# Layer 2's feed forward: 19 of 22 up projections as seven half-size block products

## The chip, the cores and the metric

One core of one Trainium2 chip. The time is device microseconds (us) of the whole program, median of three runs; the profile is of one further execution. Engines: PE is TensorE (PEld its weight loads), DVE is VectorE, ACT is ScalarE, POOL is GpSimd, SP issues the transfers.

## The reference

Two layers over 512 latent and 256 context tokens of 1024 features. Each layer mixes tokens and then runs a gated feed forward. Layer 2 computes only the latent tokens, and of it this case concerns the feed forward:

```python
def conv_ffn(h, w_up, conv_w, conv_b, w_down):
    u = h @ w_up
    u = lax.conv_general_dilated(u, conv_w[:, None, :], window_strides=(1,), padding=((1, 1),),
                                 dimension_numbers=('NWC', 'WIO', 'NWC'),
                                 feature_group_count=u.shape[-1]) + conv_b
    a, g = jnp.split(u, 2, axis=-1)
    return (jax.nn.silu(a) * g) @ w_down
```

`w_up` is 1024 x 5632, `w_down` 2816 x 1024, all float32. The convolution runs over three neighbouring tokens, separately for each of the 5632 columns.

## The kernel before

Matrix products keep float32 accuracy with two reduced-precision (fp32r) parts of each operand, h (the rounded value) and l (the rest): each product is three matmuls, h by h, l by h and h by l. The parts are made by a *split*: ACT casts the value to h, and DVE or POOL subtracts h from the value (L477 and L478 in `weight`).

The feed forward (`ffn`) takes the 2816 inner features in 22 blocks j of 128. For one j, `up` handles a *pair* of column blocks of `w_up`, s = 0 for a and s = 1 for the gate's factor. SP loads each block (128 partitions x 8 k x 128, L474), ACT and DVE split it (L477, L478), and PE forms [128 features x 512 tokens] in PSUM, with the weights stationary and the normed features X moving (L1340). In layer 2 that is 2 x 8 x 3 matmuls over 512 columns; for the first two j the 512 columns are two halves, so that work starts before all tokens are there:

```python
ps.append(([(cring.next()[:, 0:256], 0, 512, 256)] if need else []) + ([(pl, 0, 0, 256), (pl, 256, 256, 256)] if j < JS else [(pl, 0, 0, 512)]))
```

The convolution reads PSUM: ACT writes tap 1 and the bias to `cb` (L1345), and DVE adds the two shifted taps (L1346, L1347), each from PSUM and `cb`. Then ACT applies SiLU (L1350), POOL multiplies by the other half (L1351), and ACT and DVE split the product (L1352, L1353). The rows of `w_down` for j are loaded (L1327), cast by ACT (L1329) and split by POOL (L1330).

The blocks form groups of 3, 3, 3, 3, 3, 3 and 4. For a group, `down` multiplies the gated features by the rows of `w_down` for 4 token tiles and 2 halves of the output columns (L488 to L490 in `mm3`; 24 matmuls over 512 columns per j), and DVE adds the 8 results of a group to `fa` (ACT copies those of the first group, L1402; L1404 after). Ahead of each group's down products stands the up projection of the first j of the next group:

```python
pend.append(step(groups[gi + 1][0]))
...
pend += [step(j) for j in groups[gi + 1][1:]]
```

`last_group` does the last down products, and the residual and output follow.

Buffers in layer 2: four raw buffers (two of them `more_raw`), up to six weight buffers (`wr` and `more`, each h and l of 1024 values per partition), one raw buffer and four split ones for the down weights, six for gated features. The features X come from `to_features` (L632, L633 split them), which leaves the unsplit values in the output projection's buffer `mo`. The order of instructions in each engine's queue is fixed when the program is built: a planner lists them by its own cost estimates, and each engine then works through its queue in that order; only layer 2's output projection, ahead of this feed forward, follows an order written by hand. What is not in PSUM lies in SBUF (`arena_f`, `arena_r` and the zones in the profile's names).

## Time and profile before

| | before |
|---|---|
| median of 3 runs | 1800.18 us |
| lowest to highest run | 1798.51 to 1802.9 us |
| span of the profiled execution, first to last instruction | 1798.2 us |
| mean granted TensorE clock (1 is full) | 0.990 |
| PE busy | 1730.8 us (96%) |
| DVE, ACT, POOL busy | 1158.1, 790.7, 540.7 us |
| feed forward of layer 2, first up projection to the end | 1417.3 to 1798.2 us |

The profiled execution's own device time isn't given apart from its span; the span is 0.3 us under the lowest run. Busy time counts what an engine records as running, waits inside an instruction included. Matmuls overlap in the records, so their cost is read from the distance between starts. A row names its line, its engine, the operation, what it writes and reads, the shapes and the count. Behind a row, "idle before" and an arrow say how long the engine stood still before it and what ended that.

### The profile page before, as it was taken

The page shows a single profiled execution, that of the slowest core. Times are in us where ns is not written, and L with a number is a line of the kernel's source. Part 1 is how long each engine was busy: PE and PEld are TensorE (multiplying, and loading weights), DVE is VectorE, ACT ScalarE, POOL GpSimd, SP SyncE. Part 2 cuts the span into 40 slices and gives each one's busy share as a digit, 9 for nine tenths or more (in the row PEclk, how much of TensorE's full clock was granted, in tenths as well). Part 3 has the DMA queues.
Part 4 walks back from the last instruction along what each step waited for, and adds up shares of the span by engine and source line. Part 5 has one row for each costly group of instructions (what it writes and reads, how often), then busy time and mean ns, then how long its engine had stood idle before and what let it go on. Part 6 is the DMA issues. An engine that isn't in the chain of part 4 may idle for free.

```text
span 1798.2 us, 29093 instructions
## 1 busy us (share of the span) xinstructions
PE 1730.8 (96%) x11226; PEld 1450.7 (81%) x11226; DVE 1158.1 (64%) x2356; ACT 790.7 (44%) x1650; POOL 540.7 (30%) x485
## 2 busy tenths in 40 slices
PE   6999999999999999999999998999899999999997
PEld 4888865779898888878788878888778988888886
DVE  5548974662778699775666484499764664545444
ACT  5645444773553323132222355553874553333322
POOL 1325453541330202011120252245542232222223
PEclk9999999999999999999999999999999999999999
DMA  8310144003433335363433332111104353332202
GB/s 312 100 48 25 60 141 153 1 11 107 159 125 111 101 116 152 94 189 93 145 114 92 103 133 73 48 48 48 36 1 138 133 155 102 106 94 82 82 27 91
DMA packets 165582, 177.77 MB, mean 99 GB/s; under 512 B 6998, under 2 KB 137256, under 8 KB 165188
## 3 DMA queue, kind: packets, MB, share of 16 engines
q1 hardware_dynamic: 165156, 173.56, 31.0%
q0 software_dynamic: 288, 2.36, 0.4%
q8 instruction: 88, 1.44, 0.4%
q14 instruction: 50, 0.41, 0.1%
HBM read 165.38 MB, written 10.51 MB: 98 GB/s over the span
## 4 chain that ended last, share of the span: by engine, by line
PE 77%; DVE 13%; DMA 4%; issue 3%; ACT 2%; POOL 0%; DVEq 0%; ACTq 0%; POOLq 0%
PE psum L1340 31%; PE psum L488 10%; PE psum L489 10%; PE psum L490 10%; PE psum L1109 4%; PE psum L1088 3%; DMA arena_f<-in_w_mod 2%; PE psum L1061 2%; PE psum L1062 2%; DVE arena_r L478 1%; PE psum L364 1%; DVE arena_f L1197 1%; DVE arena_f L929 1%; DVE arena_f L423 1%; DMA zone_Z<-in_w_mod 1%
## 5 line engine op out<-in xcount | busy, mean ns | idle before, releaser
L1340 PE MATMUL psum<-zone_Z,arena_r 128*128 128x256 f32 (+1 forms) x2760 | 516.0, 343 | 5.5 <-DVE arena_f L1347 3.8
L1340 PEld LDWEIGHTS psum<-zone_Z,arena_r 128*128 128x128 f32 x2760 | 436.0, 189 | 75.1 <-issue 4.5
L489 PE MATMUL psum<-arena_r,zone_Z 128*128 128x256 f32 (+2 forms) x1124 | 342.2, 305 | 3.6 <-POOL zone_Z L633 2.6
L488 PE MATMUL psum<-arena_r,zone_Z 128*128 128x256 f32 (+2 forms) x1124 | 342.3, 306 | 1.9 <-ACT zone_Z L550 1.0
L490 PE MATMUL psum<-arena_r,zone_Z 128*128 128x256 f32 (+2 forms) x1124 | 341.0, 304 | 0.0
L488 PEld LDWEIGHTS psum<-arena_r,zone_Z 128*128 128x128 f32 x1124 | 212.4, 189 | 18.2 <-issue 6.2
L489 PEld LDWEIGHTS psum<-arena_r,zone_Z 128*128 128x128 f32 x1124 | 213.0, 190 | 17.2 <-issue 3.7
L490 PEld LDWEIGHTS psum<-arena_r,zone_Z 128*128 128x128 f32 x1124 | 212.6, 190 | 13.8 <-issue 5.4
L478 DVE TENSOR_TENSOR arena_r<-arena_f,arena_r 128x1024 fp32r<-128x1024 f32 (+1 forms) x111 | 159.0, 1435 | 87.2 <-ACT arena_r L477 84.8
L477 ACT CAST arena_r<-arena_f 128x1024 fp32r<-128x1024 f32 (+1 forms) x114 | 118.7, 1049 | 145.1 <-PE psum L1340 110.8
L423 DVE SCALAR_TENSOR_TENSOR arena_f<-arena_f 128x256 f32<-128x256 f32 (+1 forms) x224 | 138.8, 657 | 39.3 <-DMA arena_f<-in_w_mod 38.9
L1351 POOL TENSOR_TENSOR arena_f<-arena_f 128x768 f32<-128x768 f32 (+1 forms) x44 | 75.6, 1717 | 278.4 <-DVE arena_f L1347 251.6
L1404 DVE TENSOR_TENSOR arena_f<-arena_f,psum 128x512 f32<-128x512 f32 x100 | 68.2, 683 | 104.9 <-PE psum L490 104.8
L1330 POOL TENSOR_TENSOR arena_r<-arena_f,arena_r 128x1024 fp32r<-128x1024 f32 x22 | 53.8, 2444 | 266.9 <-ACT arena_r L1329 266.9
L1076 POOL TENSOR_SCALAR arena_f<-arena_f 128x768 f32<-128x768 f32 (+3 forms) x96 | 80.1, 837 | 93.5 <-DVE arena_f L1075 90.8
L1073 DVE TENSOR_REDUCE arena_f<-psum 128x1 f32<-128x768 f32 (+4 forms) x120 | 91.1, 767 | 21.8 <-PE psum L1062 20.2
L1330 POOL TENSOR_TENSOR zone_Z<-arena_f,zone_Z 128x1024 fp32r<-128x1024 f32 x22 | 53.9, 2452 | 162.1 <-ACT zone_Z L1329 161.8
L1345 ACT ACTIVATE arena_f<-psum,arena_f 128x512 f32<-128x512 f32 (+1 forms) x132 | 89.0, 701 | 27.8 <-PE psum L1340 27.8
L1346 DVE SCALAR_TENSOR_TENSOR arena_f<-psum,arena_f 128x511 f32<-128x511 f32 (+1 forms) x132 | 84.1, 652 | 20.3 <-ACT arena_f L1345 20.3
L1340 PE MATMUL psum<-zone_Z 128*128 128x512 f32 (+1 forms) x408 | 86.9, 366 | 0.7 <-POOL zone_Z L633 0.6
L1347 DVE SCALAR_TENSOR_TENSOR arena_f<-psum,arena_f 128x511 f32<-128x511 f32 (+1 forms) x132 | 84.8, 655 | 1.5
L1350 ACT ACTIVATE arena_f<-arena_f 128x768 f32<-128x768 f32 (+1 forms) x44 | 32.5, 739 | 120.8 <-DVE arena_f L1347 120.8
(289 smaller groups left out, 3142.9 us busy)
## 6 DMA issues: line engine op xcount, KB each, us to landing
arena_f<-in_ffn_w_up SPq DMA_DIRECT2D x88, 512.0 KB
arena_f<-in_w_mod SPq DMA_DIRECT2D x112, 256.0 KB
arena_f<-in_ffn_w_down SPq DMA_DIRECT2D x44, 512.0 KB
zone_Z<-in_w_mod SPq DMA_DIRECT2D x36, 512.0 KB
arena_f<-in_w_in SPq DMA_DIRECT2D x24, 512.0 KB
arena_f<-in_w_out SPq DMA_DIRECT2D x16, 512.0 KB
xd<-arena_f SPq DMA_DIRECT2D x16, 512.0 KB
arena_f<-xd SPq DMA_DIRECT2D x14, 512.0 KB
```

The lines of the kernel that those rows point to most:

```text
L423: nc.vector.scalar_tensor_tensor(av[:, r], x[:, i], s, av[:, r], ALU.mult, ALU.add)
L477: nc.scalar.copy(hr, rv)
L478: (nc.vector if lo == "v" else nc.gpsimd).tensor_tensor(lr, rv, hf, ALU.subtract)
L488: mm(out, lh, rh, start=first, stop=False)
L489: mm(out, ll, rh, start=False, stop=False)
L490: mm(out, lh, rl, start=False, stop=last)
L1073: nc.vector.tensor_reduce(st[:, 0:1], ps[:, 0:w], AX.X, ALU.max, negate=True)
L1330: nc.gpsimd.tensor_tensor(wp.r[:, 1], rd.f, wp.f[:, 0], ALU.subtract)
L1340: nc.tensor.matmul(p[:, po:po + n], us[s][wi][:, k], X.r[:, xi, k, o:o + n], start=(k == 0 and (wi, xi) == (0, 0)), stop=(k == KT - 1 and ...
L1345: nc.scalar.activation(d, p, AF.Identity, bias=ci[:, 3:4], scale=ci[:, 1:2])
L1346: nc.vector.scalar_tensor_tensor(d[:, 1:n], p[:, 0:n - 1], ci[:, 0:1], d[:, 1:n], ALU.mult, ALU.add)
L1347: nc.vector.scalar_tensor_tensor(d[:, 0:n - 1], p[:, 1:n], ci[:, 2:3], d[:, 0:n - 1], ALU.mult, ALU.add)
```

## The change

From j = 3 on (JD = 3), layer 2's up projection goes through `up7`. The 1024 features are cut into two halves and the 512 tokens into two halves, so the pair of column blocks (s = 0, 1) by feature halves is a 2 x 2 block matrix A, and X is a 2 x 2 block matrix B (`Quad`, four blocks of 512 features x 256 tokens). The product has seven block products in place of eight: four operands on the weights' side are sums (s1 to s4, POOL), four on the tokens' side (T1 to T4) are made once in `token_forms`, half on DVE and half on POOL. Each product is 4 k x 3 matmuls over 256 columns. Three PSUM banks per pair take the products, some accumulating in one bank; ACT copies two results and DVE adds five into `u`, in SBUF, from where the convolution now reads. `gated` is the old end of `up`, cut out as a function.

The buffers change with it: two raw buffers in place of four, four weight buffers of which a pair takes three, two half buffers in the place of a block of X that is no longer read, `fa` in the place of `mo`, four gated buffers. The raw weights are read by one DVE split, one POOL split and the four sums. Pair j = 2 uses two halves of 256 columns, as j = 0 and 1 did. Comments that the diff also removes, the freeing of buffers and `to_features` writing through `Quad.part` are left out here.

```diff
-JS, JL, NLATE = 2, 2, 6
+JS, JD, JL, NLATE = 2, 3, 2, 6
...
+class Quad:
...
+    def __init__(self, mem, at):
+        self.b = [[mem.alloc(2, 4, 256, at=at) for _ in range(2)] for _ in range(2)]
+
+    def part(self, ks, o):
+        b, k, o = self.b[ks.start // 4][o // 256], ks.start % 4, o % 256
+        return (a[:, :, k:k + ks.stop - ks.start, o:] for a in (b.r, b.f))
...
         if not need:
-            self.more = [R.alloc(2, D, at=["Z2"]) for _ in range(2)] + [R.alloc(2, D, at=["Z1"], top=True)]
+            self.forms = [R.alloc(2, 4, 256, at=["Z2"]) for _ in range(2)]
+            self.more = [Buf(R, b.zone, b.ap, b.off, b.n, (2, D)) for b in self.forms] + [R.alloc(2, D, at=["Z1"], top=True)]
...
-        gr = Ring(R, 6, 2, nt)
+        gr = Ring(R, 6 if need else 4, 2, nt)
...
-        fa = F.alloc(NT if need else 4, D)
+        fa = F.alloc(NT, D) if need else self.mo
...
+        js = JS if need else JD
...
-            if j < JS:
+            if j < js:
                 mms.sort(key=lambda m: (m[1][2] + 256) % 768)
             for s, (p, po, o, n), k, wi, xi in mms:
-                nc.tensor.matmul(p[:, po:po + n], us[s][wi][:, k], X.r[:, xi, k, o:o + n], start=(k == 0 and (wi, xi) == (0, 0)), stop=(k == KT - 1 and wi == 1))
+                x = X.r[:, xi, k, o:o + n] if need else X.b[k // 4][o // 256].r[:, xi, k % 4]
+                nc.tensor.matmul(p[:, po:po + n], us[s][wi][:, k], x, start=(k == 0 and (wi, xi) == (0, 0)), stop=(k == KT - 1 and wi == 1))
...
+        def token_forms():
...
+            z = fa.f.rearrange("p (h t) (x k n) -> p h x t k n", h=2, x=2, k=4)
+            b11, b12, b21, b22 = z[:, 0, 0], z[:, 1, 0], z[:, 0, 1], z[:, 1, 1]
+            t1, t2 = (R.alloc(2, 4, 256) for _ in range(2))
+            t3, t4 = self.forms
+            for eng, d, x, y, o in ((nc.vector, b11, b12, b11, t1), (nc.gpsimd, b12, b22, b12, t3), (nc.vector, b22, b22, b11, t2), (nc.gpsimd, b21, b21, b22, t4)):
+                eng.tensor_tensor(d, x, y, ALU.subtract)
+                r, f = (a.rearrange("p i k (t n) -> p i t k n", t=2) for a in (o.r, o.f))
+                nc.scalar.copy(r[:, 0], d)
+                eng.tensor_tensor(r[:, 1], d, f[:, 0], ALU.subtract)
+            st["T"] = [t1, t2, t3, t4]
+
+        def room():
...
+            b12 = X.b[0][1]
+            for b in self.more_raw:
+                b.free()
+            self.raw.bufs, self.raw.k = self.raw.bufs[2:], 0
+            st["big"] = [*wr, more[2]]
+            st["half"] = [b12.part(0, 2, 512), b12.part(1024, 2, 512)]
+            st["S"] = [F.alloc(2, 512) for _ in range(2)]
+            st["u"] = Ring(F, 2, 2, 512)
+            st["c1"] = Ring(F, 2, 256)
+            st["ps"] = PRing(self.PS, [(b ^ 4, 1) for b in (6, 7, 4, 5, 0, 1)])
+            st["k"] = 0
+
+        def split(raw, buf, n, eng):
...
+            hr, hf, lr = buf.r[:, 0, 0:n], buf.f[:, 0, 0:n], buf.r[:, 1, 0:n]
+            nc.scalar.copy(hr, raw)
+            eng.tensor_tensor(lr, raw, hf, ALU.subtract)
...
+        def up7(j):
...
+            raw = [self.raw.next().f for _ in range(2)]
+            for s in range(2):
+                c0 = s * FD + j * P
+                nc.sync.dma_start(raw[s][:, 0:1024].rearrange("p (k n) -> p k n", k=KT), io["ffn_w_up"][L, :, c0:c0 + P].rearrange("(k p) n -> p k n", p=P))
+            a11, a12, a21, a22 = (raw[s][:, i:i + 512] for s in range(2) for i in (0, 512))
+            big = [st["big"][(st["k"] * 3 + i) % len(st["big"])] for i in range(3)]
+            half = st["half"][st["k"] % 2]
+            st["k"] += 1
+            s12, s34 = st["S"]
+            s1, s2, s3, s4 = s12.f[:, 0], s12.f[:, 1], s34.f[:, 0], s34.f[:, 1]
+            A = {}
+            A[1], A[2] = split(raw[0][:, 0:1024], big[0], 1024, nc.vector)
+            nc.gpsimd.tensor_tensor(s1, a21, a22, ALU.add)
+            nc.gpsimd.tensor_tensor(s2, s1, a11, ALU.subtract)
+            A[5], A[6] = split(s12.f.rearrange("p s n -> p (s n)"), big[1], 1024, nc.vector)
+            nc.gpsimd.tensor_tensor(s3, a11, a21, ALU.subtract)
+            nc.gpsimd.tensor_tensor(s4, a12, s2, ALU.subtract)
+            A[7], A[3] = split(s34.f.rearrange("p s n -> p (s n)"), big[2], 1024, nc.gpsimd)
+            A[4], = split(a22, half, 512, nc.gpsimd)
+            rd, wp = rawd.next(), wd.next()
+            nc.sync.dma_start(rd.f, io["ffn_w_down"][L, j * P:(j + 1) * P, :])
+            nc.scalar.copy(wp.r[:, 0], rd.f)
+            nc.gpsimd.tensor_tensor(wp.r[:, 1], rd.f, wp.f[:, 0], ALU.subtract)
+            T = st["T"]
+            B = {1: X.b[0][0], 2: X.b[1][0], 3: X.b[1][1], 4: T[3], 5: T[0], 6: T[1], 7: T[2]}
+            pa, pb, pc = (st["ps"].next()[:, 0:256] for _ in range(3))
+
+            def product(i, ps, first):
+                h, l = A[i]
+                x = B[i].r
+                for k in range(4):
+                    for w, xi in ((h, 0), (l, 0), (h, 1)):
+                        nc.tensor.matmul(ps, w[:, k], x[:, xi, k], start=first and k == 0 and xi == 0 and w is h, stop=k == 3 and xi == 1, skip_group_check=True)
+            u, c1, cb = st["u"].next().f, st["c1"].next().f, cr.next().f
+            add = nc.vector.tensor_tensor
+            c11, c12, c21, c22 = (u[:, s, i:i + 256] for s in range(2) for i in (0, 256))
+            product(1, pa, True)
+            nc.scalar.copy(c1, pa)
+            product(6, pb, True)
+            add(c12, c1, pb, ALU.add)
+            product(5, pc, True)
+            add(c22, c1, pc, ALU.add)
+            product(2, pa, False)
+            nc.scalar.copy(c11, pa)
+            product(7, pb, False)
+            add(c22, c22, pb, ALU.add)
+            product(3, pc, False)
+            add(c12, c12, pc, ALU.add)
+            product(4, pb, False)
+            add(c21, c1, pb, ALU.add)
+            for s in range(2):
+                ci, d, x, n = cw[:, :, s * NJ + j], cb[:, s], u[:, s], 512
+                nc.scalar.activation(d, x, AF.Identity, bias=ci[:, 3:4], scale=ci[:, 1:2])
+                nc.vector.scalar_tensor_tensor(d[:, 1:n], x[:, 0:n - 1], ci[:, 0:1], d[:, 1:n], ALU.mult, ALU.add)
+                nc.vector.scalar_tensor_tensor(d[:, 0:n - 1], x[:, 1:n], ci[:, 2:3], d[:, 0:n - 1], ALU.mult, ALU.add)
+            return gated(cb), wp
...
-            r = up(j)
+            r = up(j) if need or j < JD else up7(j)
```

## Rows read from the trace of the kernel before

**Rows 1.** The page, parts 1 and 4: busy times, and the chain's lines.

```profile
PE 1730.8 (96%) x11226; PEld 1450.7 (81%) x11226; DVE 1158.1 (64%) x2356; ACT 790.7 (44%) x1650; POOL 540.7 (30%) x485
...
PE psum L1340 31%; PE psum L488 10%; PE psum L489 10%; PE psum L490 10%; PE psum L1109 4%; PE psum L1088 3%; DMA arena_f<-in_w_mod 2%; PE psum L1061 2%; PE psum L1062 2%; DVE arena_r L478 1%; PE psum L364 1%; DVE arena_f L1197 1%; DVE arena_f L929 1%; DVE arena_f L423 1%; DMA zone_Z<-in_w_mod 1%
```

**Rows 2.** Busy times by stretch (us), layer 2's feed forward in three stretches.

```profile
core 0: us, PE busy (x) PEld busy (x) DVE busy (x) ACT busy (x) POOL busy (x), PEclk, DMA share, GB/s
1417.30:1451.00 33.70, 33.01 (x243) 31.10 (x242) 23.53 (x35) 21.84 (x35) 12.96 (x8) 1.00 0.54 159
1451.00:1770.00 319.00, 319.00 (x1382) 259.01 (x1381) 155.07 (x175) 110.71 (x144) 77.88 (x41) 1.00 0.27 85
1770.00:1798.20 28.20, 17.73 (x77) 13.96 (x75) 17.12 (x30) 7.80 (x22) 9.55 (x7) 0.85 0.25 93
```

**Rows 3.** TensorE's timeline: start, us covered, line, shape, count merged in the row.

```profile
1449.71 10.65 PE L1340 MATMUL psum<-zone_Z,arena_r 128*128 128x512 f32 x45
...
1429.15 2.92 PE L1340 MATMUL psum<-zone_Z,arena_r 128*128 128x256 f32 x23
...
1252.01 0.28 PE L490 MATMUL psum<-arena_r,zone_Z 128*128 128x256 f32 x1
...
1254.50 0.28 PE L490 MATMUL psum<-arena_r,zone_Z 128*128 128x256 f32 x1
```

**Rows 4.** Instructions by source line, from 1400 us on: ns min/median/max (L1268: whole run).

```profile
L478 DVE TENSOR_TENSOR arena_r<-arena_f,arena_r x22: 1212/2012/2657, 1399.0 to 1710.8; 128x1024 fp32r<-128x1024 f32 x22
...
L1351 POOL TENSOR_TENSOR arena_f<-arena_f x22: 1281/1296/2286, 1444.5 to 1767.9; 128x512 f32<-128x512 f32 x22
...
L1347 DVE SCALAR_TENSOR_TENSOR arena_f<-psum,arena_f x44: 734/749/752, 1439.1 to 1767.0; 128x511 f32<-128x511 f32 x44
...
L1353 DVE TENSOR_TENSOR zone_Z<-arena_f,zone_Z x18: 675/691/2395, 1452.0 to 1769.9; 128x512 fp32r<-128x512 f32 x18
...
L1268 DVE TENSOR_TENSOR arena_f<-psum,arena_f x20: 409/424/425, 420.5 to 1392.5; 128x256 f32<-128x256 f32 x20
```

**Rows 5.** Timelines of POOL (L1330, L1351) and DVE (L1353, L478): start, us.

```profile
1451.42 2.41 POOL L1330 TENSOR_TENSOR zone_Z<-arena_f,zone_Z 128x1024 fp32r<-128x1024 f32 x1
...
1451.98 2.40 DVE L1353 TENSOR_TENSOR zone_Z<-arena_f,zone_Z 128x512 fp32r<-128x512 f32 x1 [1.84 <-ACT zone_Z L1352]
...
1458.70 2.41 POOL L1330 TENSOR_TENSOR arena_r<-arena_f,arena_r 128x1024 fp32r<-128x1024 f32 x1 [4.87 <-ACT arena_r L1329]
...
1459.60 2.58 DVE L478 TENSOR_TENSOR arena_r<-arena_f,arena_r 128x1024 fp32r<-128x1024 f32 x1 [2.64 <-ACT arena_r L477]
...
1463.55 1.22 DVE L478 TENSOR_TENSOR arena_r<-arena_f,arena_r 128x1024 fp32r<-128x1024 f32 x1
...
1463.78 2.13 POOL L1351 TENSOR_TENSOR arena_f<-arena_f 128x512 f32<-128x512 f32 x1 [2.67 <-DVE arena_f L1347]
```

**Rows 6.** L423 (layer 1's modulation): ns min/median/max; timelines of DVE and POOL.

```profile
L423 DVE SCALAR_TENSOR_TENSOR arena_f<-arena_f x224: 466/478/2628, 504.7 to 972.7; 128x256 f32<-128x256 f32 x84, 128x512 f32<-128x512 f32 x28
...
512.02 3.43 DVE L423 SCALAR_TENSOR_TENSOR arena_f<-arena_f 128x256 f32<-128x256 f32 x3 [0.64 <-DMA arena_f<-in_w_mod]
...
512.14 2.62 POOL L1330 TENSOR_TENSOR zone_Z<-arena_f,zone_Z 128x1024 fp32r<-128x1024 f32 x1 [7.47 <-ACT zone_Z L1329]
```

**Rows 7.** SP's timeline, one issue; then busy times by stretch, last column GB/s.

```profile
1481.75 0.37 SPq L474 DMA_DIRECT2D arena_f<-in_ffn_w_up  x1
...
1482.00:1484.00 2.00, 2.00 (x10) 1.65 (x9) 1.13 (x2) 1.22 (x2) 0.00 (x0) 1.00 0.47 134
1484.00:1486.00 2.00, 2.00 (x10) 1.63 (x10) 0.00 (x0) 0.59 (x1) 0.00 (x0) 1.00 0.43 128
```

**Rows 8.** DVE's timeline: the last features of layer 2's feed forward.

```profile
1429.98 1.29 DVE L633 TENSOR_TENSOR zone_Z<-arena_f,zone_Z 128x512 fp32r<-128x512 f32 x2 [1.26 <-ACT zone_Z L632]
```

**Rows 9.** TensorE's timeline, one gap; busy times of the stretch behind it.

```profile
1260.92 0.58 PE L1061 MATMUL psum<-arena_r 128*128 128x256 f32 x1 [2.82 <-ACT zone_Z L1074]
...
1262.00:1270.00 8.00, 7.33 (x55) 6.18 (x55) 6.08 (x21) 5.42 (x14) 6.46 (x10) 0.85 0.00 0
```

More of the change, by code (lines that the diff above doesn't have):

```diff
@@ L631, in to_features @@
         for k4 in (slice(4, 8), slice(0, 4)):
-            h = nc.scalar.copy(X.r[:, 0, k4, off:off + P], zv[:, k4])
-            l = (nc.vector if fast else nc.gpsimd).tensor_tensor(X.r[:, 1, k4, off:off + P], zv[:, k4], X.f[:, 0, k4, off:off + P], ALU.subtract)
+            xr, xf = X.part(k4, off) if isinstance(X, Quad) else (X.r[:, :, k4, off:], X.f[:, :, k4, off:])
+            h = nc.scalar.copy(xr[:, 0, :, 0:P], zv[:, k4])
+            l = (nc.vector if fast else nc.gpsimd).tensor_tensor(xr[:, 1, :, 0:P], zv[:, k4], xf[:, 0, :, 0:P], ALU.subtract)
         self.done[t] = [h, l] if fast else [h, l, e]
@@ L1297, in out_proj @@
         self.wr.k = 0
-        for b in (mo, gb, sq, junk, self.xr, *self.hl):
+        self.mo = mo
+        for b in (gb, sq, junk, self.xr, *self.hl):
             b.free()
@@ L1306, in ffn @@
         nt = NTOK if need else NLAT
+        if not need:
+            self.rc.free()
         wd = Ring(R, 4, 2, D)
         wd.bufs.append(wd.bufs.pop(0))
-        gr = Ring(R, 6, 2, nt)
+        gr = Ring(R, 6 if need else 4, 2, nt)
+        if need:
+            self.mo.free()
         rawd = Ring(F, 1, D)
-        fa = F.alloc(NT if need else 4, D)
+        fa = F.alloc(NT, D) if need else self.mo
         cr = Ring(F, 2, 2, nt)
         lring = self.banks(L, 6, 7, 4, 5)
+        js = JS if need else JD
         cring = self.banks(L, 0, 1)
@@ L1334, in up @@
                 pl = lring.next()
-                ps.append(([(cring.next()[:, 0:256], 0, 512, 256)] if need else []) + ([(pl, 0, 0, 256), (pl, 256, 256, 256)] if j < JS else [(pl, 0, 0, 512)]))
+                ps.append(([(cring.next()[:, 0:256], 0, 512, 256)] if need else []) + ([(pl, 0, 0, 256), (pl, 256, 256, 256)] if j < js else [(pl, 0, 0, 512)]))
             mms = [(s, p, k, wi, xi) for s in range(2) for k in range(KT) for wi, xi in ((0, 0), (0, 1), (1, 0)) for p in ps[s]]
-            if j < JS:
+            if j < js:
                 mms.sort(key=lambda m: (m[1][2] + 256) % 768)
             for s, (p, po, o, n), k, wi, xi in mms:
-                nc.tensor.matmul(p[:, po:po + n], us[s][wi][:, k], X.r[:, xi, k, o:o + n], start=(k == 0 and (wi, xi) == (0, 0)), stop=(k == KT - 1 and wi == 1))
+                x = X.r[:, xi, k, o:o + n] if need else X.b[k // 4][o // 256].r[:, xi, k % 4]
+                nc.tensor.matmul(p[:, po:po + n], us[s][wi][:, k], x, start=(k == 0 and (wi, xi) == (0, 0)), stop=(k == KT - 1 and wi == 1))
             for s in range(2):
@@ L1353, in up @@
             nc.vector.tensor_tensor(g.r[:, 1], a, g.f[:, 0], ALU.subtract)
-            return g, wp
+            return g
+        st = {}
+        def token_forms():
[9 more added lines that the diff above has]
+            st["T"] = [t1, t2, t3, t4]
@@ new lines, in split @@
+        def split(raw, buf, n, eng):
+            hr, hf, lr = buf.r[:, 0, 0:n], buf.f[:, 0, 0:n], buf.r[:, 1, 0:n]
+            nc.scalar.copy(hr, raw)
+            eng.tensor_tensor(lr, raw, hf, ALU.subtract)
+            return [(hr[:, i:i + 512].rearrange("p (k n) -> p k n", k=4), lr[:, i:i + 512].rearrange("p (k n) -> p k n", k=4)) for i in range(0, n, 512)]
+        def up7(j):
+            if not st:
+                token_forms()
+                room()
+            raw = [self.raw.next().f for _ in range(2)]
[52 more added lines that the diff above has]
+                nc.vector.scalar_tensor_tensor(d[:, 0:n - 1], x[:, 1:n], ci[:, 2:3], d[:, 0:n - 1], ALU.mult, ALU.add)
+            return gated(cb), wp
@@ L1389, in ffn @@
                 rawd.free(), cr.free()
+                for b in (*st["S"], st["c1"]) if st else ():
+                    b.free()
                 gb = self.load_g(L, 1)
                 self.xr = Ring(F, 3, D)
-                junk = [gr.next(), gr.next()]
+                junk = [gr.next(), gr.next()] if need else st["u"].bufs
             if last:
@@ L1405, in ffn @@
             pend += [step(j) for j in groups[gi + 1][1:]]
-        for b in (wd, gr, fa, gb, self.xr, *more, *self.more_raw):
+        for b in (wd, gr, fa, gb, self.xr, *([*st["T"], st["u"], more[2]] if st else [])):
             b.free()
@@ L1537, in run @@
             self.zone(zf, F32R)
-            X = R.alloc(2, KT, NTOK if need else NLAT, at=[zf])
+            X = R.alloc(2, KT, NTOK, at=[zf]) if need else Quad(R, [zf])
             self.out_proj(L, X)
@@ L1545, in run @@
                 self.zone(zf, F32)
-        X.free()
+        for b in X.b[0] + X.b[1]:
+            b.free()
         self.zone("Z1", None)
```

3 lines of the change are left out of this document (2 added, 1 removed).

## The prediction

> **What bounds the kernel now.** I began with the page's first and fourth parts: the share of the span that each engine is busy, and the chain of waits followed back from the end [rows 1]. TensorE is busy for 96% of the span, and the largest link of the chain is L1340, the up projection of both layers; the change rewrites it in layer 2. Next I cut the feed forward of layer 2 into three stretches [rows 2]. From 1451 to 1770 us PE is busy for all 319.0 of 319.0 us at a granted clock of 1.00, the upper level (2.4 GHz), while DVE has work for 155.07, ACT for 110.71 and POOL for 77.88 us. So in this stage only PE sets the time: a matmul taken away is worth what it costs, provided that the work put on other engines stays behind it. The last stretch, 28.2 us, is the tail behind the last pair and is not touched.
>
> **PE, part by part.** What counts is the spacing of matmul starts, since their recorded spans overlap. A merged row of 45 matmuls over 512 columns covers 10.65 us; less the last one's pipeline end (0.39) that is 10.26/44 = 0.233 us. I take 0.231, since a few records can be missing. For 256 columns with a new stationary tile each time, 23 matmuls cover 2.92 us, (2.92-0.28)/22 = 0.120, and elsewhere 21 steps take 2.49 us, 0.119 [rows 3]. Old pair: 2 outputs x 8 k x 3 passes = 48 x 0.231 = 11.09 us. New pair: 7 products x 4 k x 3 passes = 84 x 0.120 = 10.08 us. The saving is 1.01 us a pair and 19.2 us for 19, not an eighth of the stage (26 us), because two halves cost 0.240 against 0.231. Pair 2 also goes to halves (JD = 3): 96 x 0.120 - 11.09 = +0.4. If PE stays the bound the sum is -18.8 us.
>
> The Trainium skill's page "TensorE: Matmul & The Clock Gate" (Part 1, on the gap of 56 ns) puts a warm matmul at its columns over 2.4 GHz plus about 2.5 ns. By it an estimate would be 48 x 0.216 = 10.4 against 84 x 0.109 = 9.2, some 22.5 us in all; the rows above show a larger cost for each, so it is not used.
>
> **What is added on DVE, POOL and ACT.** Prices are medians of the same shapes [rows 4], and 1.22 and 2.41 us for the 1024-wide ones, as they stand alone [rows 5]. POOL, per new pair: four 512-wide sums (s1 to s4), the 512-wide split of A4 and the gate product, 6 x 1.29, and the 1024-wide splits of A7/A3 and of the down weights, 2 x 2.41, together 12.6 us; before, one of each size, 3.7. DVE: two 1024-wide splits 2 x 1.22, four convolution steps 4 x 0.75, the gate's split 0.69, and five 256-wide adds from PSUM 5 x 0.42 (L1268 has that shape), 8.2 us, and as before eight 512-wide adds of the down projection per group. ACT gets some 2.5 us more per pair and had two thirds of the stretch free [rows 2]: costed at nothing. Taken one by one, every engine is under PE's new 10.08 + 24 x 0.231 = 15.62 us per pair. That is where the sum by engines would stop.
>
> **They can't be taken one by one.** Look at the spread in [rows 4]: the split on DVE (L478) takes 1.21 us at best, 2.01 in the median into arena_r and 2.66 at worst. Beside POOL's rows the reason shows [rows 5]. POOL has a 1024-wide operation from 1458.70 to 1461.11; DVE's split starts inside it at 1459.60 and ends at 1462.18, 1.08 us after POOL is done, whatever had passed before. The 512-wide L1353 ends 0.55 us after the POOL operation it met. The other way round, POOL's L1351 starts at 1463.78 inside a split that ends at 1464.77 and needs 1.14 us from there. So a DVE operation that reads two SBUF operands and a POOL operation wait for each other whole. L1347, which reads PSUM and one SBUF operand, never exceeds 0.752 us. The multiply-add of layer 1's modulation (L423) has both operands in SBUF, and three of them (0.48 us each alone) take 3.43 us when they meet POOL [rows 6]. This decides it: the new convolution has its input in SBUF (`u`) instead of PSUM, so its four steps join those that exclude POOL.
>
> The time that one pair asks of this shared path, recorded durations: POOL 12.6 + DVE 2 x 1.22 + 4 x 0.75 + 0.69 = 6.1, **18.7 us**. With only the time that each holds the other off (1.15 and 2.26 on POOL, which is 0.14 off the recorded; 1.08 and 0.55 on DVE): 6 x 1.15 + 2 x 2.26 + 2 x 1.08 + 5 x 0.55 = **16.3 us**. PE asks 15.62; the old pair took 11.09 + 5.54 = 16.63. So both ends are above PE's new need, and the shared path becomes the bound. The Trainium skill's page "SBUF — State Buffer" (section "SBUF: two separate sides") speaks against the change in the same way: VectorE with two SBUF inputs and GpSimd take a port pair by an exclusive lock for the whole instruction. By that the pair costs the upper end; the rows agree on the exclusion and show a remainder somewhat shorter than an operation alone.
>
> I take 18.5 us per pair. 16.3 would need the next operation always ready on both engines, and the edit cuts the cover: raw weights are one pair deep (two buffers in place of four), so the next load goes out only after s4 and A4 have read. A load takes 4.25 us from issue to the last bytes (1481.75 to about 1486) [rows 7]; a pair fills three of four weight buffers, so A5/A6 and A7/A3 come only one pair ahead, once an earlier product has let go; POOL waits for three ACT casts per pair. DVE is in order too: an add that frees a PSUM bank can stand behind a split that waits for POOL (2.6 us), and the last product reuses a bank with one product (1.44 us) between, so PE can stand up to 2.6 + 0.42 - 1.44 = 1.6 us there. Against the old 16.63 that is 19 x 1.87 = **+35.5 us**; the PE saving is inside it, unused. Upper bound: 18.7 plus those 1.6 and one add of 0.42 in which nobody uses the shared path, 20.7, +77 us; lower: 16.63, PE's loss just balanced, 0.
>
> **The start.** The four token forms are four differences and four splits 1024 wide, half on each engine: POOL 4 x 2.41, DVE 4 x 1.22, 14.5 us of the shared path. They need all features, which are there at 1431.27 [rows 8], and pair 3's products need them; PE came to these at 1451 before. In 1417 to 1451 DVE and POOL together were busy 36.5 of 33.7 us [rows 2], so little room is there. I take +10 (0 if the first pairs' matmuls cover all, 14.5 if nothing does).
>
> **Edits at nothing.** The same bytes are loaded by the same descriptors, later; SP has nothing behind them but the down weights. The feature tiles written in four blocks take the same casts and subtractions. The gate ring of 4 instead of 6 holds the group and the one ahead. Memory that is freed or shared costs a wait only at pair 3: A1/A2 goes where pair 2's weights lie, inside the 10 us above.
>
> **Sum:** 35.5 + 10 = 45.5 us on a profiled span of 1798.2, which is 2.0 under the median of the runs (1800.18), a distance that I keep: **1846 us**.
>
> **Rivals.** *PE stays the bound, faster.* 1800.2 - 18.8 = 1781. It decides from the point where a pair's shared work fits into 15.62 us; against it stand 16.3 at best and 18.7 as recorded, for it only that down stretches (16.6 us per group) leave room to work ahead, and that is in the 15.62 already. Chance 0.08. *Just balanced.* Holds overlap perfectly and the forms hide: -18.8 + 19 x 0.7 + 5 to 10, about 1800 to 1805. Chance 0.06. *Latency on top of the shared path.* The loop load, sums, split, product, buffer free doesn't run full; PE then stands a few us at a time. An idle of 2.82 us at 1260.92 was followed by a mean clock of 0.85 over 8 us, part of it at the lower level (1.2 GHz) [rows 9], 1.2 us more per such gap. At 21 us a pair: 19 x 4.4 + 14.5 = +98, 1898. Chance 0.14. *The forecast*, 1806 to 1892: 0.72. That the change doesn't cut the matmuls is no rival: 84 for 96 halves stand in the loops.
>
> **Numbers.** A measurement here tells some 0.3%, 5.4 us, from no change. Faster 0.08; same (1795 to 1805.6) 0.05; slower 0.87, the rest of the balanced case in it. Range 1806 to 1892: the bounds 0 and +77 on the pairs with 6 and 14.5 for the start, leaving out the first two rivals and most of the third.
>
> **What would show it.** Right: gaps on PE in L1340's successor lines in layer 2, ended by DVE or POOL, and PE under full in 1451 to 1815; POOL up by about 19 x 8.9 + 9.6 = 178 us; convolution steps with durations up to 2 to 3 us; 54 to 57 us per group of three pairs where 50 were. Wrong: a PE without gaps, or gaps ended by the weights' DMA. It would fail if DVE's steps don't wait for POOL, or if the order of the queues keeps the two apart well enough for 16.3.

## The result, and the profile after

The changed kernel takes **1829.41 us** (median of 4 runs, 1824.83 to 1830.05) where the kernel before took 1799.96 beside it: 1.0157 times the time, 95% interval 1.0142 to 1.0171. The forecast was 1846, between 1806 and 1892. The profiled execution, that of the shortest of the four runs, spans 1823.1 us, 24.9 more than before's 1798.2.

First the page, which answers to [rows 1], and the stretch that answers to the middle of [rows 2] (PE, PEld, DVE, ACT, POOL busy, granted clock, DMA share, GB/s).

```profile
PE 1723.7 (95%) x11958; PEld 1478.3 (81%) x11958; DVE 1287.6 (71%) x2455; ACT 837.0 (46%) x1730; POOL 753.5 (41%) x603
```

```profile
1451.00:1770.00 319.00, 294.09 (x1970) 267.91 (x1969) 263.38 (x259) 148.83 (x212) 267.94 (x149) 0.99 0.30 90
...
1464.00:1467.00 3.00, 3.00 (x9) 2.14 (x7) 3.00 (x2) 1.12 (x2) 3.00 (x2) 0.52 0.07 14
```

PE has lost 25 of 319 us in a stage where it had none to lose, and DVE and POOL, each under half busy before, are now recorded as busy for 83 and 84%. The second row, of the same view, is used at the end. The instructions by source line say why (ns min/median/max): the convolution steps (L1473, L1474), 734/749/752 when they read PSUM [rows 4], read SBUF now, as do the sums on POOL (L1432).

```profile
L1473 DVE SCALAR_TENSOR_TENSOR arena_f<-arena_f x38: 735/1570/2817, 1479.2 to 1792.7; 128x511 f32<-128x511 f32 x38
...
L1474 DVE SCALAR_TENSOR_TENSOR arena_f<-arena_f x38: 740/1246/2918, 1480.7 to 1793.5; 128x511 f32<-128x511 f32 x38
...
L1412 DVE TENSOR_TENSOR arena_r<-arena_f,arena_r x28: 1212/1982/3411, 1463.5 to 1761.4; 128x1024 fp32r<-128x1024 f32 x28
...
L1432 POOL TENSOR_TENSOR arena_f<-arena_f x19: 1282/1712/2295, 1411.8 to 1755.1; 128x512 f32<-128x512 f32 x19
```

The five largest waits of TensorE from pair 3 to pair 21 (us in total, times, longest), where before's only entry for the whole feed forward is one wait of 0.6 us for L633:

```profile
PE psum L1452 <- DVE arena_f L1459: 9.2, 5, 2.6
PE psum L499 <- DVE arena_f L1527: 4.8, 5, 2.3
PE psum L500 <- DVE zone_Z L1376: 2.9, 3, 1.5
PE psum L1452 <- DVE arena_f L1461: 2.3, 2, 1.5
PE psum L1452 <- DVE arena_r L1412: 1.2, 1, 1.2
```

L1459 and L1461 are the adds that empty the banks of products 6 and 5, which products 7 and 3 take next; L1527 is the add that empties a down bank, L1376 the gate's split, L1412 the split of weights: all on DVE.

**Where the 25 us are.** Profiled executions reach this feed forward at different times (its first row scaling, L617 before and L628 after, starts at 1404.75 before, at 1402.48 after, and between 1401 and 1411 in the runs below, with the work ahead of it unchanged). So I count from that row on. A *stall* here is what the distance between two matmul starts has over its usual 0.120 us (256 columns) or 0.2325 (512), summed where it is over 0.06.

| us from the first row scaling | before | after | u in PSUM | u in PSUM, held |
|---|---|---|---|---|
| last modulation of the features | 23.6 | 30.6 | 29.8 | 23.6 |
| end of pairs 0 to 2 on PE | 49.6 | 57.0 | 56.1 | 51.0 |
| stalls between pair 2 and pair 3 | 0 | 4.4 | 4.7 | 3.1 |
| first matmul of pair 3 | 49.9 | 64.3 | 63.8 | 57.1 |
| stalls from pair 3 to the last pair's end | 0 | 30.3 | 9.5 | 13.3 |
| last matmul of pair 21 | 360.2 | 387.6 | 370.3 | 367.5 |
| down matmuls still to do then | 96 | 77 | 60 | 60 |
| end of the program | 393.5 | 420.6 | 400.6 | 397.7 |

So after is 27.1 us longer from there (2.3 were gained ahead of it, within the spread just named): 7.0 until the features are ready, 0.4 for pair 2 in halves, 4.4 of stalls ahead of pair 3; then, in the pairs, 30.3 of stalls against 19.4 of matmuls saved; and 4.2 in the tail, which is as long as before though 19 of its down matmuls (19 x 0.231 = 4.4) have been done earlier.

The tail's 77 matmuls run without a stall. Its first result is added (L1558) 10.3 us behind the start of the last product's last matmul, 11.2 before, and from there to the end it is 22.6 us, 22.1 before: the matmuls done earlier weren't on the path. The chain that ended last goes there through VectorE and a reload of a residual tile (it starts at 1813.33); TensorE had started its last matmul at 1807.93. Before, too, the chain leaves TensorE 18.9 us ahead of the end. A row of VectorE's timeline and a piece of the changed kernel's chain:

```profile
1800.45 2.48 DVE L1558 TENSOR_TENSOR arena_f<-arena_f,psum 128x512 f32<-128x512 f32 x4 [3.42 <-PE psum L501]
...
1813.33 4.44 DMA arena_f<-xd
```

The features are a part I had not costed. Timelines of the changed kernel, DVE, POOL and PE:

```profile
1426.17 2.26 DVE L276 SCALAR_TENSOR_TENSOR arena_f<-arena_f 128x1 f32<-128x1 f32 x1 [0.92 <-ACT arena_f L274]
1428.46 1.19 DVE L277 SCALAR_TENSOR_TENSOR arena_f<-arena_f 128x1 f32<-128x1 f32 x1
1429.69 1.72 DVE L628 TENSOR_SCALAR arena_f<-arena_f 128x1024 f32<-128x1024 f32 x1
...
1411.77 1.28 POOL L1432 TENSOR_TENSOR arena_f<-arena_f 128x512 f32<-128x512 f32 x1
1413.14 1.09 POOL L1433 TENSOR_TENSOR arena_f<-arena_f 128x512 f32<-128x512 f32 x1
...
1426.02 2.40 POOL L1412 TENSOR_TENSOR arena_r<-arena_f,arena_r 128x1024 fp32r<-128x1024 f32 x1 [3.28 <-ACT arena_r L1411]
1428.37 2.48 POOL L645 TENSOR_TENSOR zone_Z<-arena_f,zone_Z 128x512 fp32r<-128x512 f32 x2
...
1431.46 1.09 PE L633 MATMUL psum<-arena_f 128*128 128x128 f32 x8 [2.94 <-DVE arena_f L628]
...
1463.62 0.50 PE L500 MATMUL psum<-arena_r,zone_Z 128*128 128x512 f32 x1 [1.71 <-DVE zone_Z L1376]
```

The planner has put pair 3's sums and its A7/A3 split (L1432, L1433, L1412) between the token tiles. L276, an operation on one value per partition that takes 0.22 us where it meets nothing, starts inside POOL's split and ends at 1428.43, when the split ends (1428.42). TensorE stands 2.94 us for the scaling (L628) behind it. The last row belongs to the stalls ahead of pair 3: the planner sends 12 of group 0's down matmuls first, and they wait for pair 2's gate.

### The profile page after: what moved, and what is told of

Same layout as the page of the kernel before. It is cut to its first block, busy times and chain, and to the rows that moved or that the text cites. A ratio compares the mean times of both kernels' runs of the same rounds, so it can differ in the third digit from the quotient of the medians.

```text
span 1823.1 us, 30913 instructions
## 1 busy us (share of the span) xinstructions
PE 1723.7 (95%) x11958; PEld 1478.3 (81%) x11958; DVE 1287.6 (71%) x2455; ACT 837.0 (46%) x1730; POOL 753.5 (41%) x603
## 3 DMA queue, kind: packets, MB, share of 16 engines
q1 hardware_dynamic: 165156, 173.56, 29.8%
## 5 line engine op out<-in xcount | busy, mean ns | idle before, releaser
L1360 PE MATMUL psum<-zone_Z,arena_r 128*128 128x256 f32 (+1 forms) x2352 | 408.8, 329 | 7.0 <-DVE arena_f L1367 5.3
L1360 PEld LDWEIGHTS psum<-zone_Z,arena_r 128*128 128x128 f32 x2352 | 352.4, 189 | 54.1 <-issue 6.3
L500 PE MATMUL psum<-arena_r,zone_Z 128*128 128x256 f32 (+2 forms) x1188 | 369.8, 312 | 7.4 <-DVE zone_Z L1376 4.6
L499 PE MATMUL psum<-arena_r,zone_Z 128*128 128x256 f32 (+2 forms) x1188 | 369.1, 313 | 7.4 <-DVE arena_f L1527 4.5
L501 PE MATMUL psum<-arena_r,zone_Z 128*128 128x256 f32 (+2 forms) x1188 | 368.4, 311 | 0.0
L499 PEld LDWEIGHTS psum<-arena_r,zone_Z 128*128 128x128 f32 x1188 | 226.3, 191 | 25.8 <-issue 7.0
L500 PEld LDWEIGHTS psum<-arena_r,zone_Z 128*128 128x128 f32 x1188 | 227.3, 191 | 22.8 <-DVE zone_Z L1376 5.6
L501 PEld LDWEIGHTS psum<-arena_r,zone_Z 128*128 128x128 f32 x1188 | 226.8, 191 | 16.1 <-issue 5.4
L434 DVE SCALAR_TENSOR_TENSOR arena_f<-arena_f 128x256 f32<-128x256 f32 (+1 forms) x224 | 138.4, 656 | 35.5 <-DMA arena_f<-in_w_mod 35.1
L489 DVE TENSOR_TENSOR arena_r<-arena_f,arena_r 128x1024 fp32r<-128x1024 f32 (+1 forms) x92 | 123.4, 1343 | 53.7 <-ACT arena_r L488 53.6
L1452 PE MATMUL psum<-zone_Z,arena_r 128*128 128x256 f32 x1032 | 137.3, 284 | 10.7 <-DVE arena_f L1459 6.8
L1452 PEld LDWEIGHTS psum<-zone_Z,arena_r 128*128 128x128 f32 x1032 | 132.3, 190 | 16.5 <-DVE arena_f L1459 7.7
L1527 DVE TENSOR_TENSOR arena_f<-arena_f,psum 128x512 f32<-128x512 f32 x100 | 67.8, 682 | 60.6 <-PE psum L501 60.5
L1376 DVE TENSOR_TENSOR zone_Z<-arena_f,zone_Z 128x512 fp32r<-128x512 f32 (+1 forms) x40 | 58.9, 1473 | 36.2 <-ACT zone_Z L1375 36.2
L1086 ACT ACTIVATE arena_f<-psum,arena_f 128x768 f32<-128x768 f32 (+4 forms) x96 | 71.6, 748 | 24.3 <-DVE arena_f L1085 17.3
L1073 PE MATMUL psum<-arena_r 128*128 128x256 f32 (+1 forms) x216 | 74.7, 361 | 5.9 <-ACT zone_Z L1086 3.4
L1121 PE MATMUL psum<-arena_f,zone_Z 128*64 128x256 f32 (+1 forms) x576 | 79.5, 379 | 0.7 <-DVE arena_r L1043 0.7
```

The lines of the kernel that those rows point to most:

```text
L434: nc.vector.scalar_tensor_tensor(av[:, r], x[:, i], s, av[:, r], ALU.mult, ALU.add)
L489: (nc.vector if lo == "v" else nc.gpsimd).tensor_tensor(lr, rv, hf, ALU.subtract)
L499: mm(out, lh, rh, start=first, stop=False)
L500: mm(out, ll, rh, start=False, stop=False)
L501: mm(out, lh, rl, start=False, stop=last)
L1121: mm(ps[64 * d:64 * d + 64, a:b], at["v" + ty].f[:, k, (h + d) // 3], pts[d].f[:, i, a:b], start=(i == 0), stop=(i == len(union) - 1), til ...
```

## The experiments

Theory: DVE operations that read two SBUF operands and POOL's operations exclude each other, the new work overfills that shared path, and TensorE waits. Rivals that the rows leave open: DVE's in-order queue is simply longer; the product banks are too few; the weight buffers or the token forms delay the start. A ratio is the time over that of the kernel before measured beside the run, with its 95% interval.

**1. The sums on DVE instead of POOL.**

```diff
-            nc.gpsimd.tensor_tensor(s1, a21, a22, ALU.add)
+            nc.vector.tensor_tensor(s1, a21, a22, ALU.add)
```
(and s2 to s4 in the same way)

> The four sums s1 to s4 run on VectorE instead of GpSimd, nothing else changes. Shared path (VectorE operations with two SBUF operands and GpSimd operations exclude each other): a pair asked 18.7 us by recorded durations and took 17.4; now 18.7 - 4 x 1.29 + 4 x 0.69 = 16.3, so a period of about 15.8 to 16.4 per pair, 19 to 30 us less than the changed kernel: 1800 to 1810. Rival, VectorE's own queue is the bound and GpSimd only waits for it: 2.8 us more per pair on VectorE, so 1829 or slower, up to 1880.

Measured: 1826.14, ratio 1.0139 (1.0123 to 1.0156). A miss. By source line, then 1468 to 1786 us by stretch:

```profile
L1473 DVE SCALAR_TENSOR_TENSOR arena_f<-arena_f x38: 734/742/2912, 1489.7 to 1793.5; 128x511 f32<-128x511 f32 x38
...
L1412 DVE TENSOR_TENSOR arena_r<-arena_f,arena_r x28: 1209/1217/3399, 1465.8 to 1760.7; 128x1024 fp32r<-128x1024 f32 x28
```

```profile
1468.00:1786.00 318.00, 299.81 (x2002) 274.92 (x2001) 275.40 (x336) 148.23 (x210) 149.88 (x75) 0.98 0.33 95
```

The waits for POOL are gone from the medians (1570 to 742 ns, 1982 to 1217), and the stalls are not (29.2 us): DVE now has more work of its own, recorded as busy for 275 of 318 us (260 in the change, waits inside included). Less exclusion at the price of DVE time gives nothing.

**2. u in PSUM, so that the convolution doesn't enter the shared path.**

```diff
-            st["u"] = Ring(F, 2, 2, 512)
+            st["u"] = PRing(self.PS, [(b ^ 4, 1) for b in (5, 0, 1)])
+            st["w"] = Ring(F, 2, 2, 256)
...
-            st["ps"] = PRing(self.PS, [(b ^ 4, 1) for b in (6, 7, 4, 5, 0, 1)])
+            st["ps"] = PRing(self.PS, [(b ^ 4, 1) for b in (6, 7, 4)])
...
-            add(c12, c1, pb, ALU.add)
+            add(sc[:, 0], c1, pb, ALU.add)
...
-            add(c12, c12, pc, ALU.add)
+            add(c12, sc[:, 0], pc, ALU.add)
```
(c22 likewise; its first partial sum is the second half of `sc`, a buffer of `w`; the tail's scratch, which lay in `u`, gets buffers of its own)

> The product sums u lie in PSUM (three banks, the products then share three instead of six), so the four convolution steps read one PSUM and one SBUF operand; the same number of VectorE operations of the same width. Shared path: the steps no longer exclude GpSimd, a pair asks 18.7 - 4 x 0.75 = 15.7 us, steps at 0.75 us flat instead of 1.40 on average, period 15.8 to 16.4, 1800 to 1812. Rival, the amount of work on VectorE or the order of its queue sets the pace, not the exclusion: steps of 0.75 but the time stays within 5 us of 1829.

Measured: 1807.37, ratio 1.0035 (1.0019 to 1.0050), as expected. 22 of the 29 us are gone. By line, then by stretch:

```profile
L1475 DVE SCALAR_TENSOR_TENSOR arena_f<-psum,arena_f x38: 735/749/752, 1479.6 to 1775.5; 128x511 f32<-128x511 f32 x38
...
L1476 DVE SCALAR_TENSOR_TENSOR arena_f<-psum,arena_f x38: 734/749/752, 1480.4 to 1776.3; 128x511 f32<-128x511 f32 x38
```

```profile
1468.00:1786.00 318.00, 312.50 (x2098) 285.34 (x2099) 211.37 (x284) 156.35 (x231) 250.19 (x151) 1.00 0.33 98
```

The same steps are flat again at 0.749 us, PE is busy for 312.5 us where the changed kernel had 296.51 in that window, and the stalls fall from 30.3 to 9.5.

**3. Both edits together.**

> Both edits together: u in PSUM and s1 to s4 on VectorE. Shared path: a pair asks 13.3 us by recorded durations, less than TensorE's 15.62, so TensorE is the bound again and the period is 15.6 to 16.0; with the 12 us that the start costs: 1800 - 19 + 12 = 1793, range 1788 to 1802. Rival, latency (one pair of raw weights ahead, products waiting for adds) holds the period near 17: 1820 to 1830. Rival, VectorE full (some 12.9 us of its own per pair plus waits): 1805 to 1815.

Measured: 1835.97, ratio 1.0194 (1.0174 to 1.0213). A miss, slower than either. What DVE waited for:

```profile
DVE arena_f L1434 <- DMA arena_f<-in_ffn_w_up: 19.3, 11, 3.3
```

The sum s1 waits for raw weights that are loaded only one pair ahead. On POOL that wait is harmless (18.1 us there in run 2); on DVE the adds that empty PE's banks stand behind it. Stalls: 38.9 us.

**4. Three product banks alone,** u in SBUF as in the change: run 2 has three instead of six.

```diff
-            st["ps"] = PRing(self.PS, [(b ^ 4, 1) for b in (6, 7, 4, 5, 0, 1)])
+            st["ps"] = PRing(self.PS, [(b ^ 4, 1) for b in (6, 7, 4)])
```

> Control for the run with u in PSUM: only the products' banks are cut from six to three, u stays in SBUF. If the gain of 22 us there came from the port and not from the banks, this is as slow as the changed kernel or slower: 1829 to 1840, convolution steps still 0.74 to 2.8 us. Rival, fewer banks order VectorE's queue better: 1810 to 1820.

Measured: 1835.74 (2 runs), ratio 1.0192 (1.0164 to 1.0220). The convolution steps are as in the change:

```profile
L1473 DVE SCALAR_TENSOR_TENSOR arena_f<-arena_f x38: 739/1556/2884, 1477.6 to 1802.9; 128x511 f32<-128x511 f32 x38
```

So the gain of run 2 isn't the banks; against this control it is 28 us.

**5. One more operation into the shared path from the other side:** the A5/A6 split from DVE to POOL.

```diff
-            A[5], A[6] = split(s12.f.rearrange("p s n -> p (s n)"), big[1], 1024, nc.vector)
+            A[5], A[6] = split(s12.f.rearrange("p s n -> p (s n)"), big[1], 1024, nc.gpsimd)
```

> The split of A5 and A6 goes from VectorE to GpSimd, the reverse of the run with the sums. Theory of one shared path (sum of both engines' excluding work): a pair asks 18.7 + 1.2 = 19.9 us, so slower than the changed kernel by some 15 to 23 us, 1845 to 1852. Theory that VectorE's queue in its order is the bound (its own work, its waits for GpSimd, and what stands behind them): VectorE loses 1.22 us of work and a wait, 1815 to 1829.

Measured: 1842.63, ratio 1.0230 (1.0215 to 1.0246): 13 us slower than the change, though DVE is freed (230.22 us of 318, 259.92 in the change):

```profile
1468.00:1786.00 318.00, 294.54 (x1916) 267.90 (x1917) 230.22 (x236) 143.31 (x204) 298.06 (x162) 0.97 0.31 90
```

DVE's load alone is not the bound; this is the side of the shared path, just short of its range. But POOL is recorded as busy for 298.06 of the 318 us (262.12 in the change), so a full queue of POOL, a rival that the expectation doesn't name, would give the same.

These runs can be compared on one scale. I joined the recorded intervals of all POOL tensor operations and of DVE's tensor operations without a PSUM operand, from 1468 to 1786 us (before: 1451 to 1765): time in which someone held or awaited the shared path.

| | before | both edits | u in PSUM | sums on DVE | three banks | after | A5/A6 on POOL |
|---|---|---|---|---|---|---|---|
| share of the stretch | 40% | 70% | 84% | 86% | 92% | 94% | 98% |
| stalls of PE in the pairs, us | 0 | 38.9 | 9.5 | 29.2 | 37.2 | 30.3 | 41.8 |

With the sums on POOL the stalls are small at 84% and large from 92% on; three banks cost more than six there. The two runs with the sums on DVE stand out, above all both edits: the path is less taken than in any other run with the new form, and the stalls are almost the largest. So the share alone doesn't order the runs. That DVE's queue is the bound in those two is argued from its busy time (run 1) and its waits (run 3); no run shows it alone.

**6. No token forms.**

```diff
-                eng.tensor_tensor(d, x, y, ALU.subtract)
...
-                eng.tensor_tensor(r[:, 1], d, f[:, 0], ALU.subtract)
+                nc.scalar.copy(r[:, 1], d)
```

> Leaves out the four differences and the four subtractions of the token forms; ScalarE copies fill both parts instead, so the token operands of four products are not the right ones. All else as in the changed kernel. If the 14.5 us that the forms put on the shared path delay pair 3 (it starts at 1466.8 us, 12.2 later than before), it starts 9 to 13 us earlier and the time is 1816 to 1821. Rival, the delay comes from the weights of pair 3 and the three pairs before it, not from the forms: within 4 us of 1829.

Measured: 1820.76, ratio 1.0110 (1.0092 to 1.0128), the time as expected. Counted from the first row scaling, pair 3 starts at 56.8 us instead of 64.3, with no stall ahead of it: 7.5 us, less than the 9 to 13 expected. The features still take 28.3 us, before 23.6: the forms aren't all of the start.

**7. Other weight buffers for pair 3** (run 2, the list rotated so that its first pair doesn't take pair 2's).

```diff
-            st["big"] = [*wr, more[2]]
+            st["big"] = [wr[2], more[2], wr[0], wr[1]]
```

> u in PSUM, and pair 3 takes first the two weight buffers that pair 2 does not use. If the late start of pair 3 (1467 us against 1455 before) is the wait for pair 2's weight buffers, it starts 6 to 10 us earlier and the time is 1797 to 1802. Rival, it is the work of VectorE and GpSimd queued ahead of it: within 3 us of 1807.

Measured: 1810.97, ratio 1.0058 (1.0039 to 1.0077). A miss. Pair 3 now starts at 56.1 us, ahead of the down matmuls, and the end is where it was (400.4 us, 400.6 in run 2): the stalls moved into the pairs (14.2 for 9.5). An earlier start of pair 3 was worth nothing here.

**8. Pair 3 in the old form** (run 2 with JD = 4). Here the forms are made after group 0's down results overwrite `fa`, so they read those sums in place of the features; the work is the same.

```diff
-JS, JD, JL, NLATE = 2, 3, 2, 6
+JS, JD, JL, NLATE = 2, 4, 2, 6
...
-            st["big"] = [*wr, more[2]]
+            st["big"] = [wr[0], wr[1], wr[2], more[2]]
...
+            if j == 3 and not need:
+                self.wr.bufs, self.wr.k = [more[2], wr[2]], 0
```

> u in PSUM, and pair 3 stays with the old form (in halves), so the first pair in the new form is 4, behind the down products of the first group, and 18 pairs are in the new form; pair 3 uses the two weight buffers that pair 2 leaves. If the start costs 12 us because forms and splits crowd ahead of pair 3, most of that is hidden behind 16.6 us of down products: 1807 - 10 + 1 = 1798, range 1793 to 1802. Rival, the work is only pushed on and comes out later: 1804 to 1810.

Measured: 1814.01, ratio 1.0069 (1.0051 to 1.0087). A miss, but it shows the features at 23.6 us, as before: pair 4's sums come too late to stand among them. The stalls in the pairs are 19.3 us; the forms' late place costs them, as run 10 bears out, which moves the forms alone.

**9. Run 2 with pair 3's preparation held back** behind the last features.

```diff
+            with self.behind(2 if j == JD else None), self.behind(3 if j == JD else None):
-            A[1], A[2] = split(raw[0][:, 0:1024], big[0], 1024, nc.vector)
+                A[1], A[2] = split(raw[0][:, 0:1024], big[0], 1024, nc.vector)
```
(all lines to A4's split are indented)

> u in PSUM, and pair 3's splits and sums held back until the last features of layer 2's feed forward are written. Theory: the part of the late start that is left (pair 3 at 1467 us in nearly every variant, 1455 before) begins earlier than the token forms: the planner puts s1 to s4 and the A7/A3 split of pair 3 between the token tiles' features, where they exclude DVE's chain of row scaling and modulation. From the first row scaling of these features to the last modulation it is 23.5 us in the kernel before, 30.6 in the changed one, 29.8 with u in PSUM. Held back, that stretch should be 23.5 to 24.5 us, and the time from the first row scaling to the end of the program, 400.6 us with u in PSUM and 393.4 before, should fall to 395 to 397: 1801 to 1804 us. Rival: the same 10 us of work is only moved to where pair 3 waits for it, beside the forms and the weight splits; the stretch becomes short and the time stays within 2 us of 1807.

Measured: 1803.47, ratio 1.0028 (1.0014 to 1.0042). POOL's timeline, next to the one above:

```profile
1413.23 3.02 POOL L645 TENSOR_TENSOR zone_Z<-arena_f,zone_Z 128x512 fp32r<-128x512 f32 x2 [3.63 <-ACT zone_Z L644]
1419.88 3.05 POOL L645 TENSOR_TENSOR zone_Z<-arena_f,zone_Z 128x512 fp32r<-128x512 f32 x2 [3.63 <-ACT zone_Z L644]
1422.90 1.28 POOL L1435 TENSOR_TENSOR arena_f<-arena_f 128x512 f32<-128x512 f32 x1
```

The features are back at 23.6 us and a tile every 6.65 us, so pair 3's sums and splits among them did cost these 6.2 us. Of the total only 2.9 come back (400.6 to 397.7): pair 3 is still met by stalls, half theory, half rival.

**10. Run 8 with the forms made ahead of pair 3,** from the features.

```diff
-            if not st:
-                token_forms()
+            if "k" not in st:
                 room()
...
+            if j == 3 and not need:
+                token_forms()
+                self.wr.bufs, self.wr.k = [more[2], wr[2]], 0
```

> u in PSUM, pair 3 in the old form (JD = 4), and the token forms made ahead of pair 3 from the features, so that the 11.5 us of pair 3's matmuls cover them and pair 4's sums; 18 pairs in the new form. Theory (the start's loss is preparation without cover: pair 3's sums among the features, and the forms and splits behind them): features in 23.5 us as before, pair 4 without a gap, the lost 1 us of PE in pair 3 the only price; from the first row scaling to the end 391 to 395 us where the kernel before has 393.4, a time of 1796 to 1803. Rival: the forms now stand among the weight splits of pairs 1 to 3 on the shared path and hold up pairs 1 to 3 themselves, with gaps on TensorE ahead of pair 3 ended by the weights' splits; 398 us or more, 1805 to 1812.

Measured: 1803.11, ratio 1.0027 (1.0013 to 1.0041); from the first row scaling 396.2 us. Stalls in the pairs are down to 7.0, but 4.2 stand ahead of pair 4, and the pair left in the old form gives up its 1 us. It lies between the two ranges.

**11. Run 9 with other banks:** products in 4, 5, 0, results in 1, 6, 7.

```diff
-            st["u"] = PRing(self.PS, [(b ^ 4, 1) for b in (5, 0, 1)])
+            st["u"] = PRing(self.PS, [(b ^ 4, 1) for b in (1, 6, 7)])
...
-            st["ps"] = PRing(self.PS, [(b ^ 4, 1) for b in (6, 7, 4)])
+            st["ps"] = PRing(self.PS, [(b ^ 4, 1) for b in (4, 5, 0)])
```

> As u_psum_hold, with the PSUM banks of the new form dealt otherwise: products in 4, 5, 0 and the results in 1, 6, 7 (before 6, 7, 4 and 5, 0, 1). In u_psum_hold TensorE stood 2.52 us at pair 3's second matmul behind a convolution step of pair 2, which still read its bank (pair 2 lies in 6 and 7), and 0.89 + 1.72 us ahead of that at the first group's down products. Theory: what is left of the start is the bank that pair 3 takes from pair 2; with banks free since pair 1 these 2.5 to 5 us go: 1798 to 1801 us, no measurable difference to the kernel before. Rival: pair 3 then waits for its splits or forms, which are as late, and the time stays within 1.5 us of 1803.5.

Measured: 1804.68, ratio 1.0010 (0.9994 to 1.0027): no difference to the kernel before that can be measured, and none shown to run 9. In the profiled execution it is 396.8 us from the first row scaling to the end, 393.5 before. TensorE's timeline:

```profile
1462.45 0.50 PE L499 MATMUL psum<-arena_r,zone_Z 128*128 128x512 f32 x1 [0.88 <-ACT zone_Z L1375]
1464.67 0.80 PE L500 MATMUL psum<-arena_r,zone_Z 128*128 128x512 f32 x1 [1.72 <-DVE zone_Z L1376]
...
1470.57 2.89 PE L1455 MATMUL psum<-zone_Z,arena_r 128*128 128x256 f32 x22 [0.61 <-DVE arena_r L1414]
```

The wait for the bank is gone; the waits for pair 2's gate stand as they were, and a wait for the weights' split follows: the rival.

**12. Run 10 with other banks** (products in 6, 7, 0, results in 1, 4, 5) **and product 3 ahead of product 2.**

```diff
             add(sc[:, 1], c1, pc, ALU.add)
+            product(3, pc, False)
+            add(c12, sc[:, 0], pc, ALU.add)
             product(2, pa, False)
...
-            product(3, pc, False)
-            add(c12, sc[:, 0], pc, ALU.add)
```

> As u_psum_jd4e, with products in banks 6, 7, 0 and results in 1, 4, 5, and product 3 ahead of product 2, so that the first half (s = 0) of a pair's results is complete two products (2.9 us) before the pair's end in place of one. Theory: what is left against the kernel before is latency behind a pair's last product, at the groups' last pairs (down products waiting for the gate's splits) and in the tail, where after the last product 30 us pass with 60 to 72 down matmuls left, 96 before; the earlier half and the freed banks give 2 to 4 us back: 1799 to 1801 us. Rival: the gate's multiplication and split wait for the second half, which ends where it did: 1802 to 1805.

Measured: 1813.40, ratio 1.0057 (1.0040 to 1.0074), slower than run 10. TensorE waits 5.9 us in 4 places for L1460, the add behind product 6. Two things were changed at once, and which of them did it isn't told apart; the tail was not shortened (31.5 us with 69 down matmuls in it, 30.6 with 51 in run 10).

## Why the prediction was right, and where it was off

- *PE's saving, 19.2 us.* Right: the 19 new pairs take 212.4 us of matmul starts, 21.6 of it stalls; 190.8 against 210.2 before, 19.4. Pair 2's +0.4 is there too.
- *PE stops being the bound because the convolution's input in SBUF excludes POOL.* Right, and shown by run 2 with its control, run 4: steps of up to 2.9 us become flat at 0.749 with u in PSUM, and 22 us go, 28 against the control. The loss when one operation more goes to POOL (run 5) fits, but a full POOL queue would fit as well. The Trainium skill, "SBUF — State Buffer", section "SBUF: two separate sides", has this rule, and the trace agrees on the exclusion: L276 ended at 1428.43, the POOL split that it met at 1428.42. It isn't all of it: with the sums on DVE the path is less taken and the stalls stay (runs 1 and 3).
- *18.5 us per pair, +35.5.* The direction was right, the term too large: **the mis-sized step is the choice of 18.5 near the recorded durations.** Pair 3's start to the last matmul of pair 21 went from 310.4 to 323.3 us, +12.9 in place of +35.5, and groups of three took 50.6 to 53.7 us where I forecast 54 to 57, some 17.4 a pair. 94% of 17.4 is 16.4 us of shared path, which is my lower figure from the holds, 16.3; only about 1 us a pair passed with nobody on it, where I had allowed 2.2. The waits that I feared for one-pair-deep raw weights were small (ACT's splits waited 8.4 us in all for them in that stretch).
- *PE waits up to 1.6 us where the last product reuses a bank.* The mechanism was right, an add that frees a bank late in DVE's queue (L1459 and L1461, 11.5 us in 7 waits); the place was not. TensorE stood ahead of products 7 and 3, whose banks products 6 and 5 had filled with two products (2.9 us) between, and not ahead of the last product, 4, behind L1465; single waits reached 2.6, not 1.6.
- *Start, +10 by the token forms.* Close in sum (7.0 + 4.4 = 11.4), which is partly luck, for its reason is half wrong. (PE came to pair 3 at 1454.6 us before, not at 1451.) Without the forms pair 3 came 7.5 us earlier (run 6); but most of what was lost earlier, in the features, was pair 3's own sums and split (run 9). I had costed moved weights preparation "at nothing" by asking what waits behind it, and not where the planner would put it.
- *"The tail is not touched."* Right for its length (33.0 us, 33.2 before), but it hid a loss of about 4 us: the prediction doesn't ask what the down matmuls are worth that are done ahead of the tail. They shortened the tail by 0.3 us, since its end isn't reached through TensorE. Against the kernel before, a late gate is at most 1.3 us of this: a new pair completes both halves of its results in its last two products, where the old pair had finished its first half 24 matmuls (5.5 us) ahead, and the last gate's split ends 6.9 us behind the last product's last matmul starts, 5.6 before. Whether an earlier gate would shorten the tail isn't shown; run 12 meant to test it and didn't.
- *POOL +178 us:* +212.8, the waits inside included.

What stays open: no version beat the kernel before. Runs 9 to 11 leave 3 to 4 us of stalls ahead of the first new pair, 7 to 13 in the pairs and 5 to 8 in the tail (its length against that of the kernel before, less the down matmuls done earlier) against a saving of 18 to 19, and I did not find an order that removes them together.

## What to carry to other kernels

Moving an operand from PSUM to SBUF was not free for VectorE here: look first whether GpSimd works beside it, join the two engines' recorded intervals, and treat the result as one resource; then look at each queue by itself, for a low share of the joined path doesn't show that nothing waits. When a change shortens the bounding engine by a few per cent and adds operand preparation elsewhere, cost the first and the last instance too: where the scheduler will put the new work, and whether the end is reached through the engine that got faster at all. Compare stages from a common event on, not in absolute times.
